# Sums of weight blocks made by adding transfers instead of VectorE

## The chip, the cores and the metric

The kernel runs on one core of a Trainium2 chip. A core has TensorE (matmuls), VectorE and ScalarE (elementwise work), GpSimd (elementwise work, and it can begin transfers), and SyncE, which here begins nearly all transfers. All transfers run on the core's 16 DMA engines. The metric is the device time of one execution in microseconds (us); lower is better. Before the change the median of three runs was 892.14 us (891.55 to 892.82).

## The reference

The program is a two-layer encoder trunk on 256 positions of 1024 channels. Each layer is a feed-forward block, a token mixer (a convolution module in the first layer, latent attention in the second) and another feed-forward block; a last norm follows.

```python
def swiglu_ffn(h, w1, w3, w2):
    return (jax.nn.silu(h @ w1) * (h @ w3)) @ w2

for i in range(DEPTH):
    h = h + 0.5 * swiglu_ffn(rmsnorm(h, ffn_norm1[i]), ffn1_w1[i], ffn1_w3[i], ffn1_w2[i])
    m = rmsnorm(h, mix_norm[i])
    h = h + (conv_module(m, ...) if i % 2 == 0 else mla(m, positions, ...))
    h = h + 0.5 * swiglu_ffn(rmsnorm(h, ffn_norm2[i]), ffn2_w1[i], ffn2_w3[i], ffn2_w2[i])
return rmsnorm(h, final_norm)
```

So there are four feed-forward blocks. The inner width is 2816. All data are float32, and `w1`, `w3`, `w2` of the four blocks are most of the bytes that are read.

## The kernel before, in words

**Weight blocks.** Weights are read in blocks of 128 partitions by 2048 float32 (1 MB). A block is loaded into one of four raw tiles (`raw`, `RAW_BUFS = 4`) by SyncE. Then it is split into two float32r tiles: `hi`, a rounded copy made by ScalarE, and `lo`, the rest `raw - hi`, made by VectorE. Each is done in two halves of 1024 columns (`PIECES = 2`). There are five pairs of `hi` and `lo` (`W_BUFS = 5`), so the splitting can run at most some four blocks ahead of TensorE. A product of float32 accuracy is three float32r matmuls (`mm3`, lines 331 to 337): rows' `hi` by weights' `lo`, `hi` by `hi`, rows' `lo` by `hi`. An ordinary block is used for two tiles of 128 rows, so it is 24 matmuls of 128x512.

**Groups of seven.** In each feed-forward block two stretches of four blocks are done in another way, by the scheme of seven products in place of eight for 2x2 blocks. One lies in chunk 3 of the up projection (an "up group", `SEVEN_UP`), one at the start of the down projection (a "down group", `SEVEN_DOWN`). That makes eight groups. The four weight blocks `four[0]` to `four[3]` are the 2x2 blocks of the weights, and the rows are cut in 2x2 blocks too: `rows(a, tb)` are plain blocks of rows, `forms[0]` to `forms[3]` are sums or differences of them, made once per group by `sums_of_rows` (line 339) and split by `forms_of`. Each of the seven products multiplies one block or form of rows by one block or sum of weight blocks, 12 matmuls, and adds it to one of four banks of results, `c11`, `c21`, `c12`, `c22`.

The weight sides are made by `load_seven` (line 190). For product `j` it says what is loaded, which sums are made, and which raw tile is split. Before the change the sums are subtractions on VectorE over a whole tile (`sub`, line 201): two at `j = 1`, one at `j = 2`, one at `j = 6`. The raw tiles 11, 12, 22, 21 are fetched at `j = 0, 0, 1, 2`, and split in the order 11, 11, 11, 21, 12, 22, 11.

`seven_products` (line 373) issues the products. Between them ScalarE copies `c11` to `c21` and one product to a spare tile `kept`, and VectorE adds `c21` and `kept` into `c12` and later into `c22`. The next product into `c21` has to wait for such a copy or add.

**What sets the order.** Every engine works through its own queue in order. The order within a queue comes from a planner that runs when the program is built. `urgent` gives instructions priority there; `order(a, b)` puts `a` behind `b`; `behind` puts a split behind the last urgent instructions. `load_ahead` says how many blocks ahead of TensorE the loads and splits are issued. SyncE's queue holds the weight loads and also the turns of the gated values (`turn_blocks`, line 480), which write 32x32-transposed tiles to memory and read them back; `gates` lists the splits of the turned values. GpSimd begins no transfer before the change; it has small norm arithmetic (lines 444 to 447) and part of the convolution.

Of the kernel before, what the change touches and what calls it, by code (L numbers as in the profile page):

```python
# [11 lines left out]
F32 = mybir.dt.float32  # L12
# [7 lines left out]
P = 128  # L20
# [69 lines left out]
def trunk(ctx: ExitStack, tc: tile.TileContext, x, xt, first, pos, invf, gfin, wdw,  # L90
# [91 lines left out]

    def fetched(src):
        raw = rawp.tile([P, HB], F32, tag="raw", name=uid("raw"))
        dma = nc.sync.dma_start(raw, src)
        if turns:
            order(dma, turns[-1].ins)
        return raw

    def load_seven(j, four, b, pieces):  # L190
        hi = wp.tile([P, HB], F32R, tag="hi", name=uid("hi"))
        lo = wp.tile([P, HB], F32R, tag="lo", name=uid("lo"))
        n = len(loaded)
        if j == 0:
            b[11], b[12] = fetched(four[0]), fetched(four[1])
        elif j == 1:
            b[22] = fetched(four[3])
        elif j == 2:
            b[21] = fetched(four[2])
        def sub(out, left, right):  # L200
            ins = nc.vector.tensor_sub(out, left, right)  # L201
            behind(ins)
            return ins

        if j == 1:
            sub(b[11], b[12], b[11])
            sub(b[12], b[22], b[12])
        elif j == 2:
            thirds[n] = sub(b[11], b[22], b[11])
        elif j == 6:  # L210
            sub(b[11], b[21], b[11])
        raw = b[(11, 11, 11, 21, 12, 22, 11)[j]]
        for i in range(pieces):
            c = slice(i * HB // pieces, (i + 1) * HB // pieces)
            casts[n, i] = nc.scalar.copy(hi[:, c], raw[:, c]), sub(lo[:, c], raw[:, c], hi[:, c].bitcast(F32))  # L215
            behind(casts[n, i][0])
        return hi, lo
# [155 lines left out]
    def seven_products(xh, xl, forms, banks, late={}):  # L373


        def rows(a, tb):
            k = slice(4 * a, 4 * a + 4)
            return xh[:, k, tbs(tb)], xl[:, k, tbs(tb)]

        def product(a, b, fresh):  # L380
            load_ahead(W_BUFS - 1)
            (hi, lo), = weights(1, False)
            for k in range(4):
# [4 lines left out]
        before = []  # L388
# [5 lines left out]
        product(forms[0], c22, True)  # L394
        kept = tmp.tile([P, 512], F32, tag="s", name=uid("p5"))
        urgent(nc.scalar.copy)(kept, c22)
        product(forms[1], c21, False)
        add = urgent(nc.vector.tensor_add)(c12, c21, kept)
        order(casts[n0 + 5, 0][1], add.ins)
        for high, low in gates[-2 * NT:-NT] if not late else ():  # L400
            order(low, thirds[n0 + 2].ins)
# [3 lines left out]
        product(rows(1, 0), c11, False)  # L405
        product(forms[2], c21, False)
        add = urgent(nc.vector.tensor_add)(c22, c21, kept)
        order(casts[n0 + 6, 0][1], add.ins)
# [3 lines left out]
        product(forms[3], c12, False)  # L412
        product(rows(1, 1), c21, False)

# [65 lines left out]
    def turn_blocks(pool, src, n, tag, after=(), b=None):  # L480
# [370 lines left out]
    def ffn_in(act, X, make_next, beside, apart, seven_up, seven_down):  # L851
# [587 lines left out]
    def mla_in(act, X, make_next, cc, sn):  # L1439
# [423 lines left out]
```

## Time and profile before

| | us |
|---|---|
| median of three runs | 892.14 |
| the profiled execution's own time | 891.44 |
| its span, first to last instruction | 889.5 |
| TensorE (PE) busy | 882.0 |
| VectorE (DVE) busy | 770.4 |
| ScalarE (ACT) busy | 580.2 |
| GpSimd (POOL) busy | 104.8 |

The mean granted TensorE clock was 0.999 of full speed. The 16 DMA engines were busy for 62% of the span and moved 198.94 MB. A group of instructions in the profile is named by its line in the kernel, the engine, the operation and the tiles it writes and reads (`out<-in`); then come the count, busy time, mean nanoseconds of one, and the idle time of the engine just before them with what ended it. Matmuls overlap in the pipeline, so the 389 ns that the profile gives a matmul of 128x512 is longer than the distance from one to the next. A stage is a stretch of the span, given in us from its start.

### The profile page before, as it was taken

What the parts mean: (1) busy time and instruction counts of PE and PEld (TensorE: products, weight loads), DVE (VectorE), ACT (ScalarE), POOL (GpSimd) and SP (SyncE); (2) the same over time, 40 slices, a digit from 0 to 9 for tenths busy, and PEclk for the clock granted to TensorE, in tenths of its full rate; (3) what the DMA queues carried; (4) which work ended last, traced back from release to release, by engine and by line L of the source; (5) the groups of instructions that cost most, each with busy time, mean ns of one, the idle gap of its engine ahead of it and who ended that gap; (6) DMA issues with size and microseconds to landing.
All of it is one profiled execution on the core that took longest, in us unless ns stands there. A gap on an engine that the chain in (4) does not pass through costs nothing.

```text
span 889.5 us, 12294 instructions
## 1 busy us (share of the span) xinstructions
PE 882.0 (99%) x4209; PEld 741.9 (83%) x4209; DVE 770.4 (87%) x1114; ACT 580.2 (65%) x1005; POOL 104.8 (12%) x227
## 2 busy tenths in 40 slices
PE   9999999999999999999999999999999999999997
PEld 7888887898988888888888888888899888888886
DVE  6899999789999998999498989995778689989973
ACT  7667868789887655657275465673676666474752
POOL 1000000079952000000010000001400010000000
PEclk9999999999999999999999999999999999999999
DMA  9884929834216855939759378495643549287541
GB/s 338 297 308 161 398 80 374 300 132 153 96 60 225 307 213 194 365 93 393 251 179 344 97 249 318 142 386 183 221 147 142 190 155 368 80 300 276 192 190 48
DMA packets 71054, 198.94 MB, mean 224 GB/s; under 512 B 12368, under 2 KB 41936, under 8 KB 51664
## 3 DMA queue, kind: packets, MB, share of 16 engines
q1 hardware_dynamic: 70560, 197.47, 61.9%
q8 instruction: 33, 0.54, 0.2%
q10 hardware_dynamic: 432, 0.69, 0.2%
q14 instruction: 29, 0.24, 0.1%
HBM read 181.87 MB, written 16.25 MB: 223 GB/s over the span
## 4 chain that ended last, share of the span: by engine, by line
PE 98%; DVE 1%; issue 0%; ACT 0%; ACTq 0%; DVEq 0%
PE u L333 17%; PE u L337 17%; PE u L336 17%; PE o L333 9%; PE o L337 9%; PE o L336 9%; PE u L1019 3%; PE gate L1019 3%; PE o L1255 3%; PE u L418 2%; PE sc L1616 1%; PE tp L453 1%; PE pairs L1062 1%; DVE lo L201 1%; PE a L337 1%; PE a L336 1%
## 5 line engine op out<-in xcount | busy, mean ns | idle before, releaser
L248 DVE TENSOR_TENSOR lo<-raw,hi 128x1024 fp32r<-128x1024 f32 (+1 forms) x228 | 266.8, 1210 | 29.2 <-ACT hi L247 28.5
L247 ACT CAST hi<-raw 128x1024 fp32r<-128x1024 f32 (+1 forms) x230 | 228.5, 1044 | 72.1 <-DMA raw<-in_f2w 24.3
L337 PE MATMUL u<-hi,Xl 128*128 128x512 f32 x592 | 230.4, 389 | 0.0
L336 PE MATMUL u<-hi,Xh 128*128 128x512 f32 x592 | 230.3, 389 | 0.0
L333 PE MATMUL u<-lo,Xh 128*128 128x512 f32 x592 | 230.2, 389 | 0.0
L215 ACT CAST hi<-raw 128x1024 fp32r<-128x1024 f32 x112 | 111.7, 1049 | 56.7 <-DVE raw L201 46.4
L201 DVE TENSOR_TENSOR lo<-raw,hi 128x1024 fp32r<-128x1024 f32 x112 | 132.0, 1215 | 6.6 <-ACT hi L215 6.5
L337 PEld LDWEIGHTS u<-hi,Xl 128*128 128x128 f32 x592 | 111.1, 188 | 23.6 <-DVE Xl L472 0.5
L336 PEld LDWEIGHTS u<-hi,Xh 128*128 128x128 f32 x592 | 111.1, 188 | 23.1
L333 PEld LDWEIGHTS u<-lo,Xh 128*128 128x128 f32 x592 | 111.1, 188 | 22.9
L333 PE MATMUL o<-lo,Gh 128*128 128x512 f32 (+1 forms) x276 | 106.7, 386 | 0.0
L336 PE MATMUL o<-hi,Gh 128*128 128x512 f32 (+1 forms) x276 | 106.5, 386 | 0.0
L337 PE MATMUL o<-hi,Gl 128*128 128x512 f32 (+1 forms) x276 | 106.5, 386 | 0.0
L444 POOL TENSOR_TENSOR ms<-ss 128x1 f32<-128x1 f32 x16 | 8.1, 509 | 592.8 <-ACT junk L436 592.8
L201 DVE TENSOR_TENSOR raw<-raw,raw 128x2048 f32<-128x2048 f32 x32 | 73.1, 2285 | 0.8 <-DMA raw<-in_f1w 0.2
L333 PEld LDWEIGHTS o<-lo,Gh 128*128 128x128 f32 x276 | 51.8, 188 | 10.6 <-DVE lo L201 0.2
L337 PEld LDWEIGHTS o<-hi,Gl 128*128 128x128 f32 x276 | 51.8, 188 | 10.5
L336 PEld LDWEIGHTS o<-hi,Gh 128*128 128x128 f32 x276 | 51.8, 188 | 10.4
L1108 DVE SCALAR_TENSOR_TENSOR acc<-V,dw,acc 128x128 f32<-128x128 f32 (+1 forms) x174 | 53.9, 390 | 0.0
L970 ACT ACTIVATE s<-u,R 128x512 f32<-128x512 f32 (+1 forms) x48 | 30.9, 647 | 29.5 <-PE u L337 28.7
L1129 ACT ACTIVATE prod<-V,dw 128x128 f32<-128x128 f32 (+1 forms) x128 | 45.6, 415 | 1.9 <-POOL Y L1130 1.0
L806 DVE SCALAR_TENSOR_TENSOR h<-o,rh,h 128x512 f32<-128x512 f32 (+1 forms) x18 | 12.9, 719 | 29.0 <-PE o L337 29.0
(269 smaller groups left out, 1306.6 us busy)
## 6 DMA issues: line engine op xcount, KB each, us to landing
raw<-in_f2w SPq DMA_DIRECT2D x66, 1024.0 KB, 5.6
raw<-in_f1w SPq DMA_DIRECT2D x62, 1024.0 KB, 6.9
raw<-in_cw SPq DMA_DIRECT2D x12, 1024.0 KB, 5.2
gd<-gt SPq DMA_DIRECT2D x160, 64.0 KB, 2.9
gb<-gd SPq DMA_DIRECT2D x24, 256.0 KB, 2.8
rows<-gd SPq DMA_DIRECT2D x16, 256.0 KB, 3.3
raw<-in_wo SPq DMA_DIRECT2D x4, 1024.0 KB, 4.7
hd<-rows SPq DMA_DIRECT2D x56, 64.0 KB, 2.3
```

The lines of the kernel that those rows point to most:

```text
L201: ins = nc.vector.tensor_sub(out, left, right)
L215: casts[n, i] = nc.scalar.copy(hi[:, c], raw[:, c]), sub(lo[:, c], raw[:, c], hi[:, c].bitcast(F32))
L247: casts[len(loaded), i] = (nc.scalar.copy(hi[:, c], raw[:, c]), low.tensor_sub(lo[:, c], raw[:, c], hi[:, c].bitcast(F32)))
L248: low.tensor_sub(lo[:, c], raw[:, c], hi[:, c].bitcast(F32)))
L333: mm = nc.tensor.matmul(o, ah, bl, start=start, stop=False, skip_group_check=seeded)
L336: nc.tensor.matmul(o, ah, bh, start=False, stop=False, skip_group_check=seeded)
L337: return nc.tensor.matmul(o, al, bh, start=False, stop=stop, skip_group_check=seeded)
L970: nc.scalar.activation(s[:, :w], u[0, tb][:, :w], AF.Silu, scale=X.r[tb])
L1019: mm = nc.tensor.matmul(u[:, t], w[:, c], X.x[:, k, t], start=(k == 0), stop=(k == KT - 1))
L1108: dve_last.append(nc.vector.scalar_tensor_tensor(out if j == j1 - 1 else y, v, w, y, op0=ALU.mult, op1=ALU.add))
L1129: prods_last.append(nc.scalar.activation(p, v, AF.Copy, scale=w))
L1255: p = nc.tensor.matmul(o[tb, d], (Zl if kind == "x" else Zh)[:, f, tbs(tb)], (lo if kind == "l" else hi)[:, c], start=(f, kind) == (0, "l" ...
```

## The change

The sums of weight blocks are no longer made by VectorE. A transfer with `accum_op=ALU.add` reads a block from memory and adds it to what lies in the raw tile; it is begun from GpSimd. Since it can only add, the signs of the row forms and of the additions of results are turned (`sums_of_rows`, `tensor_sub` in `seven_products`).

For each group four raw tiles are fetched at once, in the order d = `four[2]`, y = `four[1]`, c = `four[0]`, x = `four[0]`. Two adding transfers follow: `four[3]` to y, `four[1]` to x. At product 3 `four[3]` is added to x, at product 6 `four[2]`. At product 5 `four[3]` is loaded anew into c. The tiles are split in the order x, c, d, x, y, c, x. So a group has five plain loads where it had four, and four adding transfers where it had four subtractions.

The seven products are issued in another order, and product 2 is cut into halves, with product 3 between them. Some order rules follow the new numbering; the gated values' turns get a third buffer; and the attention's scores of heads 1 and 2 are ordered behind those of the head before.

```diff
     def load_seven(j, four, b, pieces):
...
         if j == 0:
-            b[11], b[12] = fetched(four[0]), fetched(four[1])
-        elif j == 1:
-            b[22] = fetched(four[3])
-        elif j == 2:
-            b[21] = fetched(four[2])
...
-        if j == 1:
-            sub(b[11], b[12], b[11])
-            sub(b[12], b[22], b[12])
-        elif j == 2:
-            thirds[n] = sub(b[11], b[22], b[11])
+            b["d"], b["y"], b["c"], b["x"] = (fetched(four[i]) for i in (2, 1, 0, 0))
+            nc.gpsimd.dma_start(b["y"], four[3], accum_op=ALU.add)
+            nc.gpsimd.dma_start(b["x"], four[1], accum_op=ALU.add)
+        elif j == 3:
+            nc.gpsimd.dma_start(b["x"], four[3], accum_op=ALU.add)
+        elif j == 5:
+            fetched(four[3], b["c"])
         elif j == 6:
-            sub(b[11], b[21], b[11])
-        raw = b[(11, 11, 11, 21, 12, 22, 11)[j]]
+            nc.gpsimd.dma_start(b["x"], four[2], accum_op=ALU.add)
+        raw = b["xcdxycx"[j]]
...
-        sums = [(0, x22, x21, x22, ALU.add), (2, x21, x11, x21, ALU.subtract), (1, x11, x22, x11, ALU.subtract),
-                (3, x12, x12, x11, ALU.subtract)]
+        sums = [(0, x22, x21, x22, ALU.subtract), (2, x21, x11, x21, ALU.subtract),
+                (1, x11, x22, x11, ALU.subtract), (3, x12, x12, x11, ALU.add)]
...
-        product(rows(0, 0), c11, True)
-        first = urgent(nc.scalar.copy)(c21, c11)
...
+        product(0, forms[0], c22, True)
+        kept = tmp.tile([P, 512], F32, tag="s", name=uid("p5"))
+        first = urgent(nc.scalar.copy)(kept, c22)
...
+        product(1, rows(0, 0), c11, True)
+        urgent(nc.scalar.copy)(c21, c11)
+        product(2, rows(1, 0), c11, False, range(2))
+        product(3, forms[1], c21, False)
+        product(2, rows(1, 0), c11, False, range(2, 4))
+        add = urgent(nc.vector.tensor_sub)(c12, kept, c21)
+        order(casts[n0 + 6, 0][1], add.ins)
...
+        product(4, forms[2], c21, False)
+        add = urgent(nc.vector.tensor_sub)(c22, kept, c21)
+        product(5, forms[3], c12, False)
...
+        order(casts[n0 + 7, 0][1], add.ins)
+        product(6, rows(1, 1), c21, False)
...
-            b = pool.tile([P, 512], F32, tag=tag + "b", name=uid(tag + "b"), bufs=2)
+            b = pool.tile([P, 512], F32, tag=tag + "b", name=uid(tag + "b"), bufs=3 if tag == "g" else 2)
...
-            for gate in gates[-2 * NT:]:
+            for gate in gates[-2 * NT - 1:]:
...
-            last = None
+            last = score_last[-1] if 0 < hd < 3 else None
```

More of the change, by code (lines that the diff above doesn't have):

```diff
@@ L181, in raw_to, with fetched @@
             raws[len(loaded) + len(raws)] = raw, nc.sync.dma_start(raw[:, :src.shape[-1]], src)
-    def fetched(src):
-        raw = rawp.tile([P, HB], F32, tag="raw", name=uid("raw"))
+    def fetched(src, raw=None):
+        if raw is None:
+            raw = rawp.tile([P, HB], F32, tag="raw", name=uid("raw"))
         dma = nc.sync.dma_start(raw, src)
@@ L378, in rows, with product @@
             return xh[:, k, tbs(tb)], xl[:, k, tbs(tb)]
-        def product(a, b, fresh):
+        def product(j, a, b, fresh, ks=range(4)):
             load_ahead(W_BUFS - 1)
-            (hi, lo), = weights(1, False)
-            for k in range(4):
+            if ks[0] == 0:
+                parts[j], = weights(1, False)
+            hi, lo = parts[j]
+            for k in ks:
                 c = slice(k * 512, k * 512 + 512)
@@ L387, in seven_products @@
         n0 = n_used[0]
-        before = []
+        before, parts = [], {}
         c11, c21, c12, c22 = banks[0, 0], banks[1, 0], banks[0, 1], banks[1, 1]
-        product(rows(0, 0), c11, True)
-        first = urgent(nc.scalar.copy)(c21, c11)
+        product(0, forms[0], c22, True)
+        kept = tmp.tile([P, 512], F32, tag="s", name=uid("p5"))
+        first = urgent(nc.scalar.copy)(kept, c22)
         for cast in late.values():
             order(cast, first.ins)
[L394 to L399, printed above, removed]
+        product(1, rows(0, 0), c11, True)
[5 more added lines that the diff above has]
+        order(casts[n0 + 6, 0][1], add.ins)
         for high, low in gates[-2 * NT:-NT] if not late else ():
-            order(low, thirds[n0 + 2].ins)
+            order(low, casts[n0 + 2, PIECES - 1][1].ins)
         late_gates = []
```

16 lines of the change are left out of this document (4 added, 12 removed).

## The prediction

> **What bounds the kernel now.** I read the page first, then busy time by stage, then the groups' own rows. The rows of the page, with the span, busy time by engine, the share of the chain that ended last, and the costliest groups of a weight group's work (lines L201 and L215):
>
> ```profile
> span 889.5 us, 12294 instructions
> PE 882.0 (99%) x4209; PEld 741.9 (83%) x4209; DVE 770.4 (87%) x1114; ACT 580.2 (65%) x1005; POOL 104.8 (12%) x227
> ...
> q1 hardware_dynamic: 70560, 197.47, 61.9%
> ...
> PE 98%; DVE 1%; issue 0%; ACT 0%; ACTq 0%; DVEq 0%
> ...
> L215 ACT CAST hi<-raw 128x1024 fp32r<-128x1024 f32 x112 | 111.7, 1049 | 56.7 <-DVE raw L201 46.4
> L201 DVE TENSOR_TENSOR lo<-raw,hi 128x1024 fp32r<-128x1024 f32 x112 | 132.0, 1215 | 6.6 <-ACT hi L215 6.5
> ...
> L201 DVE TENSOR_TENSOR raw<-raw,raw 128x2048 f32<-128x2048 f32 x32 | 73.1, 2285 | 0.8 <-DMA raw<-in_f1w 0.2
> ```
>
> TensorE is the bound: it is on 98% of the chain. Busy time by stage says where its 7.5 idle us (889.5 - 882.0) lie; the last columns are the granted clock, the DMA engines' share and GB/s:
>
> ```profile
> 0.00:30.00 30.00, 28.96 (x130) 23.21 (x131) 18.45 (x28) 22.42 (x37) 3.79 (x19) 1.00 0.86 322
> 90.00:110.00 20.00, 20.00 (x90) 16.57 (x89) 20.00 (x24) 17.20 (x32) 0.00 (x0) 1.00 1.02 395
> 110.00:140.00 30.00, 29.60 (x129) 23.72 (x129) 29.85 (x31) 17.71 (x22) 0.00 (x0) 1.00 0.45 152
> 353.70:389.00 35.30, 35.30 (x157) 29.22 (x156) 34.57 (x35) 20.51 (x25) 0.00 (x0) 1.00 0.77 279
> 690.00:710.00 20.00, 19.98 (x100) 16.35 (x99) 12.87 (x21) 12.39 (x29) 0.00 (x0) 1.00 0.58 211
> 860.00:889.50 29.50, 23.50 (x116) 19.75 (x114) 9.61 (x17) 6.60 (x16) 1.48 (x5) 0.98 0.10 36
> ```
>
> Of the 7.5 us, 1.04 are at the start and 6.00 at the end, which the change doesn't touch; 0.40 are inside a weight group, in this one row of TensorE's timeline:
>
> ```profile
> 136.75 0.47 PE L333 MATMUL o<-lo,rows 128*128 128x512 f32 x1 [0.40 <-DVE lo L201]
> ```
>
> VectorE is nearly as full (34.57 of 35.30 us between an up group and its down group), but its work ends in time: TensorE waited for it 0.40 us in all. So freeing VectorE can buy almost nothing; whatever makes a weight block late costs in full.
>
> **The change part by part.** One: 32 subtractions go (4 in each of 8 groups), 32 x 2.285 = 73.1 us of VectorE, 9.1 us a group. Directly worth at most the 0.40 us above.
>
> Two: SyncE begins 5 loads a group instead of 4, and GpSimd 4 adding transfers. The queue that only loads moved 395 GB/s at a share of 1.02, so 1 MB (1.049 MB) takes 1.049/395 = 2.65 us of all engines. An adding transfer also reads what it adds to: between one pass (2.65) and two (5.3). A group's DMA grows by 5 to 9 passes, 13 to 24 us; eight groups make 106 to 191 us on 61.9% of 889.5 us, so 74 to 83%. The engines still have room on average; inside a group it is tight.
>
> Three, the term that decides: the sums now lie on a chain. One buffer x is loaded, added to, cast (product 0), added to again, cast (product 3), added to again, cast (product 6). These rows are the issue of the fourth raw load of each of the eight groups, in order of time, on SyncE's queue, with the landing time of all these loads:
>
> ```profile
> 56.77 0.67 SPq L185 DMA_DIRECT2D raw<-in_f1w  x1
> 105.88 0.33 SPq L185 DMA_DIRECT2D raw<-in_f1w  x1
> 314.36 0.38 SPq L185 DMA_DIRECT2D raw<-in_f2w  x1
> 372.25 0.35 SPq L185 DMA_DIRECT2D raw<-in_f2w  x1
> 488.01 0.33 SPq L185 DMA_DIRECT2D raw<-in_f1w  x1
> 547.05 0.35 SPq L185 DMA_DIRECT2D raw<-in_f1w  x1
> 751.79 0.33 SPq L185 DMA_DIRECT2D raw<-in_f2w  x1
> 809.03 0.35 SPq L185 DMA_DIRECT2D raw<-in_f2w  x1
> ...
> DMA to landing us min/median/max: 5.3/7.6/9.5
> ```
>
> And these are the matmuls that place the groups: for the up groups (u) the first of product 1, which takes its rows from Gh; for the down groups (o) the first of product 0:
>
> ```profile
> 73.33 0.39 PE L333 MATMUL u<-lo,Gh 128*128 128x512 f32 x1
> 122.29 0.39 PE L333 MATMUL o<-lo,Gh 128*128 128x512 f32 x1
> 340.13 0.39 PE L333 MATMUL u<-lo,Gh 128*128 128x512 f32 x1
> 389.09 0.39 PE L333 MATMUL o<-lo,Gh 128*128 128x512 f32 x1
> 514.21 0.39 PE L333 MATMUL u<-lo,Gh 128*128 128x512 f32 x1
> 514.44 0.39 PE L336 MATMUL u<-hi,Gh 128*128 128x512 f32 x1
> 563.17 0.39 PE L333 MATMUL o<-lo,Gh 128*128 128x512 f32 x1
> 777.11 0.39 PE L333 MATMUL u<-lo,Gh 128*128 128x512 f32 x1
> 826.07 0.39 PE L333 MATMUL o<-lo,Gh 128*128 128x512 f32 x1
> ```
>
> Matmuls start about 0.227 us apart (514.21 to 514.44; 157 in 35.30 us give 0.225), so a product of 12 is 2.72 us and an up group starts 2.72 before its row. The lead, from the fourth load's issue to product 0, is 13.8, 23.1, 23.5 and 22.6 us for the up groups and 16.4, 16.8, 16.1 and 17.0 for the down groups. In the new order x is that fourth load.
>
> Call an adding transfer, from issue to landing, L. No row shows one. The low end is the quickest landing of these loads, 5.3; the high end the slowest plus a second pass, 9.5 + 2.65 = 12.1. I take the median landing, 7.6: the same megabyte into the same tile, on engines shared with the same traffic; a second pass on an otherwise free queue would give 5.3 + 2.65 = 8.0, close by. From x's issue to the first half cast: 7.6 (load) + L + 1.05 (ACT) + 1.22 (DVE) = 9.9 + L = 17.5. From one cast of x to the next: the rest of the cast, which must have read x, 1.2; the transfer, L; the next first half, 2.3; so 3.5 + L = 11.1 us between usable blocks. TensorE wants product 3 after 2.5 products (half of product 2 is put behind it), 6.8 us, and product 6 another 3.5 products, 9.5 us, later. A group without spare lead so loses 4.3 + 1.6 = 5.9 us; spare lead is taken off.
>
> - Up groups 2 to 4: spare 23.1 - 17.5 = 5.6, 6.0, 5.1; they lose 0.3, 0, 0.8: 1.1 us.
> - Up group 1: lead 13.8, 3.7 late already; 3.7 + 5.9 = 9.6 us.
> - Down groups: by the leads above each loses about 0.9 + 5.9 = 6.8. But the fourth buffer there came free late because VectorE was full before it (34.57 of 35.30), and 9.1 us of that goes. Leads can then grow towards the 23 us that the other up groups have. I take that, since 9.1 is more than the 6 to 7 missing: 4 x 0.4 = 1.6 us. If this cover is gone they cost 27 us.
>
> Together 12.3 us. By L = 5.3 the same sum is up group 1's 1.4 + 2.0 = 3.4 us and nothing elsewhere; by 12.1, 15 us for a group without spare lead, 14 for each of the seven others and 23 for the first: 121 us.
>
> The Trainium skill, "DMA: Bandwidth & Descriptors", section "Anatomy of one DMA", gives a transfer begun from GpSimd about 2.0 us plus bytes/436 GB/s. For 1 MB my estimate by that page is 4.4 us; the whole sum would be 1.6 us. These loads, begun from SyncE, landed in 5.3 to 9.5, which is slower, and nothing here shows an adding one.
>
> Four: what is queued behind the new waits. GpSimd's adding transfers wait for x's load and then for its casts, but GpSimd ran nothing in the stages around these groups (0.00 in 353.70:389.00), so nobody waits behind them; an issue costs about 0.3 us if like SyncE's. On SyncE the reload of c waits for product 1's casts, with the gated values' turns and the next blocks' loads behind it. Those casts run well ahead of TensorE; zero, or if they slip the next loads slip with them.
>
> Five: the half of product 2, 1.36 us, covers the copy of c21 and, behind product 3, the subtraction into c12, where a whole product covered the add before. These are the copy and the two adds in up group 2:
>
> ```profile
> 340.39 0.57 ACT L259 COPY u<-u 128x512 f32<-128x512 f32 x1 [5.64 <-PE u L337]
> ...
> 346.71 0.69 DVE L259 TENSOR_TENSOR u<-u,p 128x512 f32<-128x512 f32 x1
> 351.21 0.70 DVE L259 TENSOR_TENSOR u<-u,p 128x512 f32<-128x512 f32 x1 [0.49 <-PE u L337]
> ```
>
> Product 2 ended at 345.57 and the add at 347.40, 1.83 us later: 0.5 more than the half covers. The copy ended 0.83 after its product and the second add 0.90 after its own (351.01). So 0 to 0.5 us for each of 8 groups; I take 0.1, 1 us in all.
>
> Six: the orders given to the attention scores, the third turn buffer and the gates' order add no instruction. They cost nothing as long as TensorE has queued matmuls, as it has (19.98 of 20 us in 690:710); without that cover, tenths of a us.
>
> Sum: 891.4 (the profiled execution) - 0.4 + 12.3 + 1.0 = 904.3; the median of the runs is 0.7 higher, so **905**.
>
> **The rivals.**
> Hidden: the adding transfer takes 5 us or less, x is loaded early, and TensorE stays full. For it: only 62% of DMA time is used and three up groups have 23 us of lead. Against it: up group 1 has 13.8. Time 891 to 893. By the page's 4.4 us it would be this case, at 1.6 us.
> Faster: the one mechanism is work on VectorE and ScalarE coming earlier, so that the small delays of matmuls vanish. The rows of the attention's output product, 411 ns against 392 for its middle one:
>
> ```profile
> L333 PE MATMUL o<-lo,Oh 128*128 128x512 f32 x32 | 13.2, 411 | 0.0
> L336 PE MATMUL o<-hi,Oh 128*128 128x512 f32 x32 | 12.6, 392 | 0.0
> L337 PE MATMUL o<-hi,Ol 128*128 128x512 f32 x32 | 9.7, 411 | 0.0
> ```
>
> 64 x 0.019 = 1.2 us, and the 0.40: 1.6 us, 890.5. It decides only if all of that goes and nothing is late.
> Slow transfers: L of 10 or more, because the additions go at less than half the copying rate or wait behind loads. With L = 10, a group without spare lead loses 6.7 + 4.0 = 10.7; the first 6.1 + 10.7, seven others about 7.6: 70 us, about 962. For it: the queue was full at 1.02 just before the first down group. The same page says in "Issuing engines are not separate DMA queues" that all issuers share the 16 engines. The full stretch is loads alone, so no run here shows the sharing.
> Cover gone: L as forecast, but the down groups keep their leads of 16 to 17 us because the order of casts is kept: 905 + 27 - 2 = 930.
>
> **How the numbers follow.** Forecast 42%, hidden 22%, faster 3%, slow transfers 17%, cover gone 16%. The runs spread over 891.55 to 892.82, so about 0.2% can be told from no change: 890.4 to 893.9. Hidden falls in it but for 2 parts in 100: faster 0.03, same 0.20, slower 0.77. The likeliest case alone spans 895 to 918. The range runs from 890.8, the hidden case's edge, to 945, which leaves out the far half of the slow transfers.
>
> **What would show it.** Right: TensorE idle 12 us more, in front of products 0, 3 and 6 on L333, ended by casts whose own wait is for an adding transfer; worst in the first up group; VectorE busy some 73 us less; a GpSimd queue of 32 x 1 MB landing in about 7.6 us. Wrong: landings of 10 us and more, or stalls spread over the down groups, put it higher; TensorE busy for the same 882 us with no new idle time puts it at the old time.

## The result, and the profile after

The changed kernel takes 1020.1 us (median of 4 runs, 1016.76 to 1023.19) against 892.4 for the kernel before: a ratio of 1.143, 95% interval 1.138 to 1.148. That is 128 us slower, where 12.9 were forecast and 945 was the upper end of the range.

The profiled execution has a span of 1014.7 us. These are rows of its page: busy time by engine, the DMA queues (q0 is the new one, which GpSimd fills), and the casts to `hi` of a weight group's blocks (L209):

```profile
PE 913.4 (90%) x4209; PEld 758.3 (75%) x4209; DVE 700.6 (69%) x1082; ACT 577.7 (57%) x1005; POOL 134.7 (13%) x259
...
q1 hardware_dynamic: 71712, 205.86, 56.7%
q0 software_dynamic: 4608, 33.56, 17.3%
...
L209 ACT CAST hi<-raw 128x1024 fp32r<-128x1024 f32 x112 | 109.7, 1045 | 171.6 <-DMA raw<-in_f2w 100.7
...
raw<-in_f1w POOLq DMA_DIRECT2D x16, 1024.0 KB, 9.1
...
gd<-gt SPq DMA_DIRECT2D x160, 64.0 KB, 6.0
```

VectorE did lose its 70 us (770.4 to 700.6). But TensorE is now idle for 101.3 us (1014.7 - 913.4) where it was idle for 7.5, and it is busy for 31.4 us more with the same 4209 matmuls: 93.8 + 31.4 = 125.2, which is the whole growth of the span (1014.7 - 889.5). The casts of L209 now wait for transfers. The last row is a transfer that the change doesn't touch: the 64 KB pieces of the gated values on their way through memory. In the kernel before, the same row reads:

```profile
gd<-gt SPq DMA_DIRECT2D x160, 64.0 KB, 2.9
```

The table of waits names what ended TensorE's idle time: each row has the total, the number of times and the longest. u and o are banks of the up and down groups; L329 is the first matmul of each triple, L210 the part of the casts that makes `lo`, L255 the helper of the copies and of the sums of banks.

```profile
PE u L329 <- ACT u L255: 26.0, 4, 9.9
PE o L329 <- DVE lo L210: 24.6, 5, 6.7
PE o L329 <- ACT o L255: 21.7, 4, 8.9
PE u L329 <- DVE lo L210: 9.4, 3, 6.3
PE u L329 <- DVE u L255: 6.3, 4, 1.9
PE o L329 <- DVE o L255: 5.8, 3, 4.8
```

The six rows add up to 93.8 us: 47.7 end with ScalarE's copy of a bank, 34.0 with a cast, 12.1 with a sum of banks. The copy is short, so it must have been late. The second up group shows why. First the issues on GpSimd's queue and on SyncE's, then ScalarE, then TensorE (start, duration, in brackets the idle time before and what ended it):

```profile
348.28 0.33 SPq L186 DMA_DIRECT2D raw<-in_f2w  x1
...
355.29 0.86 POOL L199 DMA_DIRECT2D raw<-in_f2w  x1 [5.42 <-DMA raw<-in_f2w]
370.71 0.86 POOL L201 DMA_DIRECT2D raw<-in_f2w  x1 [14.56 <-DVE lo L210]
...
366.86 5.81 ACT L209 CAST hi<-raw 128x1024 fp32r<-128x1024 f32 x6 [5.08 <-DMA raw<-in_f2w]
...
379.89 1.99 ACT L209 CAST hi<-raw 128x1024 fp32r<-128x1024 f32 x2 [6.19 <-DMA raw<-in_f2w]
381.79 0.58 ACT L255 COPY p<-u 128x512 f32<-128x512 f32 x1
...
384.16 0.58 ACT L255 COPY u<-u 128x512 f32<-128x512 f32 x1
...
384.79 0.79 PE L329 MATMUL u<-lo,Xh 128*128 128x512 f32 x1 [7.43 <-ACT u L255]
385.39 0.63 PE L332 MATMUL u<-hi,Xh 128*128 128x512 f32 x1
385.81 0.63 PE L333 MATMUL u<-hi,Xl 128*128 128x512 f32 x1
```

The load of x is issued at 348.28. Its first adding transfer begins at 355.29, and the sum is cast from 366.86 on: 11.6 us. The second begins at 370.71 and ends ScalarE's wait at 379.89: 9.2 us. ScalarE works in order, and the cast of block 3 stands ahead of both copies, so the copies start only when the second adding transfer has landed (a cast of block 4 then stands ahead of the second copy). Product 2 writes the bank that the second copy reads; so TensorE stands still until 384.79.

After such a stall the matmuls are 0.43 us apart (385.39 to 385.81) instead of 0.227. The window behind this stall, with granted clock, DMA share and GB/s in the last columns:

```profile
385.00:389.00 4.00, 4.00 (x10) 3.13 (x11) 4.00 (x5) 2.18 (x3) 0.21 (x1) 0.50 0.78 116
```

The granted clock is 0.50. Behind this stall 14 matmuls go at that pace, 2.8 us more than at 0.227. Most of the 31.4 us of longer busy time lie in such stretches: in TensorE's timeline, matmuls that start over 0.3 us apart without a wait cost some 26 us more than in the kernel before. A long stall is paid for again behind it.

### The profile page after: what moved, and what is told of

Same layout as the page of the kernel before. It is cut to its first block, busy times and chain, and to the rows that moved or that the text cites. A ratio compares the mean times of both kernels' runs of the same rounds, so it can differ in the third digit from the quotient of the medians.

```text
span 1014.7 us, 12381 instructions
## 1 busy us (share of the span) xinstructions
PE 913.4 (90%) x4209; PEld 758.3 (75%) x4209; DVE 700.6 (69%) x1082; ACT 577.7 (57%) x1005; POOL 134.7 (13%) x259
## 3 DMA queue, kind: packets, MB, share of 16 engines
q0 software_dynamic: 4608, 33.56, 17.3%
## 5 line engine op out<-in xcount | busy, mean ns | idle before, releaser
L329 PE MATMUL u<-lo,Xh 128*128 128x512 f32 x592 | 233.7, 395 | 32.3 <-ACT u L255 26.0
L210 DVE TENSOR_TENSOR lo<-raw,hi 128x1024 fp32r<-128x1024 f32 x112 | 131.3, 1219 | 147.5 <-ACT hi L209 147.5
L209 ACT CAST hi<-raw 128x1024 fp32r<-128x1024 f32 x112 | 109.7, 1045 | 171.6 <-DMA raw<-in_f2w 100.7
L329 PEld LDWEIGHTS u<-lo,Xh 128*128 128x128 f32 x592 | 112.3, 190 | 58.9 <-ACT u L255 27.7
L329 PE MATMUL o<-lo,Gh 128*128 128x512 f32 (+1 forms) x276 | 109.1, 397 | 26.9 <-ACT o L255 21.7
L332 PE MATMUL o<-hi,Gh 128*128 128x512 f32 (+1 forms) x276 | 108.7, 394 | 0.0
L333 PE MATMUL o<-hi,Gl 128*128 128x512 f32 (+1 forms) x276 | 108.6, 393 | 0.0
L329 PEld LDWEIGHTS o<-lo,Gh 128*128 128x128 f32 x276 | 53.1, 192 | 40.5 <-ACT o L255 23.4
L443 POOL TENSOR_TENSOR ms<-ss 128x1 f32<-128x1 f32 x16 | 10.5, 656 | 267.2 <-ACT junk L435 267.2
L329 PE MATMUL u<-lo,Gh 128*128 128x512 f32 x64 | 28.1, 438 | 9.4 <-DVE lo L210 9.4
L971 DVE TENSOR_TENSOR s<-s,u 128x512 f32<-128x512 f32 (+1 forms) x32 | 19.6, 612 | 23.4 <-PE u L333 16.2
```

The source lines that it names most:

```text
L209: casts[n, i] = (nc.scalar.copy(hi[:, c], raw[:, c]), nc.vector.tensor_sub(lo[:, c], raw[:, c], hi[:, c].bitcast(F32)))
L210: nc.vector.tensor_sub(lo[:, c], raw[:, c], hi[:, c].bitcast(F32)))
L329: mm = nc.tensor.matmul(o, ah, bl, start=start, stop=False, skip_group_check=seeded)
L332: nc.tensor.matmul(o, ah, bh, start=False, stop=False, skip_group_check=seeded)
L333: return nc.tensor.matmul(o, al, bh, start=False, stop=stop, skip_group_check=seeded)
L443: nc.gpsimd.tensor_tensor(ms[:, 0:1], ss[:, 0:1], ss[:, 1:2], op=ALU.add)
```

## The experiments

My first theory was the forecast's own, with a larger price: the series of load, add, cast, add on the one buffer x. Rivals were the copy that ScalarE makes late, the slower clock, and the traffic as such, which delays everything else that goes through the DMA engines. Times are medians of two to ten runs, with the ratio to the kernel before and its 95% interval in brackets.

### Taking the adding transfers away, or adding nothing

Without the four adding transfers of each group (the sums are left out, everything else stays):

```diff
-            nc.gpsimd.dma_start(b["y"], four[3], accum_op=ALU.add)
-            nc.gpsimd.dma_start(b["x"], four[1], accum_op=ALU.add)
...
-            nc.gpsimd.dma_start(b["x"], four[3], accum_op=ALU.add)
...
-            nc.gpsimd.dma_start(b["x"], four[2], accum_op=ALU.add)
```

> All 32 adding transfers are left out (the sums of weight blocks are not made); the five loads a group, the new order of products and the halves of product 2 stay. Theory chain (the loss is made by the series load - add - cast - add - cast - add - cast on buffer x): nearly all of the 125 us goes, 894 to 900 us; what stays is the wait of product 2 for the copy of c11, about 0.7 us in each of 8 groups. Rival order (the new order of products and of the queues makes the loss): 940 us or more.

Measured: 905.6 us, 1.0150 [1.0133, 1.0166]. That lies between the two expectations. So 114 of the 128 us hang on the adding transfers. The other 13 are a cost of the new order alone, and TensorE's row of the second down group says where:

```profile
402.33 0.50 PE L323 MATMUL o<-lo,Gh 128*128 128x512 f32 x1 [1.38 <-ACT o L249]
```

Product 2 waits for the copy of the bank into which it goes on adding; in the up groups it does so for 0.66 to 2.12 us. In all eight groups that is 9.6 us.

The same transfers with the same bytes, copying instead of adding:

```diff
-            nc.gpsimd.dma_start(b["y"], four[3], accum_op=ALU.add)
+            nc.gpsimd.dma_start(b["y"], four[3])
```

(and so for all four)

> The 32 transfers stay on GpSimd with all their waits, but copy instead of adding (the sums are not made). If the adding itself is dear (the second pass, 2.65 us each): landings fall from about 9 to about 6.5 us, two or three steps of the chain a group, 950 to 975 us. If a transfer begun from GpSimd is slow whatever it does: landings stay at 8 to 9 us and the time above 1000 us.

Measured: 939.7 us, 1.0531 [1.0478, 1.0584]. That is below both expectations. All waits and the order of issue are as in the changed kernel, and 80 us are gone. The rows of this run on the new queue:

```profile
q0 software_dynamic: 4608, 33.56, 10.0%
...
raw<-in_f1w POOLq DMA_DIRECT2D x16, 1024.0 KB, 5.6
raw<-in_f2w POOLq DMA_DIRECT2D x16, 1024.0 KB, 6.4
```

17.3% of 1014.7 us by 32 is 5.5 us of all 16 engines for one adding transfer; 10.0% of its span of 941.6 by 32 is 2.9 for a copying one. Landing falls from 9.1 to about 6 us. This run changes two things at once, the load on the engines and the length of the series; later runs part them.

### Is it the late copy, or the series on x?

The casts of block 3 and the lower half of block 6's are put behind the copy and behind the sum of banks:

```diff
+        taken = urgent(nc.scalar.copy)(c21, c11)
+        for i in range(PIECES):
+            order(casts[n0 + 3, i][0], taken.ins)
...
+        for i in range(PIECES):
+            order(casts[n0 + 6, i][1], add.ins)
```

> The changed kernel, with ScalarE's cast of product 3 behind the copy of c21, and VectorE's part of product 6 behind the subtraction into c22. TensorE waited 47.7 us for such copies and 11.7 us for such subtractions. Theory queue (copies stuck behind casts that wait for a transfer cost their whole wait): 955 to 970 us. Theory chain (the cast that they wait behind is needed next anyway): only the half of product 2 moves into the wait, 8 to 25 us gained, 992 to 1010 us.

Measured: 1021.3 us, 1.1446 [1.1402, 1.1490]. Nothing was won; both expectations were lower. TensorE's waits for ScalarE's copies fell from 47.7 to 14.7 us, and its waits for casts rose from 34.0 to 69.8: what had been waited for behind the copy is waited for at product 3.

The same, with x loaded first and its adding transfer begun first:

```diff
-            b["d"], b["y"], b["c"], b["x"] = (fetched(four[i]) for i in (2, 1, 0, 0))
+            b["x"], b["c"], b["d"], b["y"] = (fetched(four[i]) for i in (0, 0, 2, 1))
+            nc.gpsimd.dma_start(b["x"], four[1], accum_op=ALU.add)
             nc.gpsimd.dma_start(b["y"], four[3], accum_op=ALU.add)
-            nc.gpsimd.dma_start(b["x"], four[1], accum_op=ALU.add)
```

> As copy_first, and x is fetched first instead of last and its first addition comes first in GpSimd's queue. Theory chain: the 28 us of waits in front of product 0, with the slow clock behind them, vanish, 30 to 40 us below copy_first; the waits in front of product 3 stay or grow. If the wait for x's first addition is not what makes product 0 late: no change against copy_first.

Measured: 989.8 us, 1.1093 [1.1071, 1.1115]. Loading x last costs some 31 us. Next, products 0 and 1 are exchanged, without the two orders on casts above, so that the copied bank is finished a product earlier and the copy has a whole product to itself; x is then needed a product later, too. This was run with x first and all adding transfers, and without any adding transfer and with the loads in the changed kernel's order:

```diff
-        raw = b["xcdxycx"[j]]
+        raw = b["cxdxycx"[j]]
...
-        product(0, forms[0], c22, True)
+        product(0, rows(0, 0), c11, True)
...
+        first = urgent(nc.scalar.copy)(c21, c11)
...
-        product(1, rows(0, 0), c11, True)
+        product(1, forms[0], c22, True)
...
-        urgent(nc.scalar.copy)(c21, c11)
+        urgent(nc.scalar.copy)(kept, c22)
```

> All 32 adding transfers and all sums right; products 0 and 1 in swapped places (the copy of c11 is covered, x is needed one product later) and x fetched first. Theory chain: the waits in front of the first product of x mostly go, those in front of products 3 and 6 stay: 940 to 975 us. If the waits for copies and subtractions were most of the loss: 900 to 920 us.

> As no_add (the sums of weight blocks are not made), but products 0 and 1 change places, and with them the casts: the plain rows first, so that the copy of c11 to c21 lies beside the product into c22 and not in front of product 2, which writes c11. If that copy makes what no_add still lost (13 us): 891 to 896 us. If the fifth load, the halves of product 2 or the changed queues make it: stays at 902 to 907 us.

Measured: 976.9 us with x first and all adding transfers, 1.0938 [1.0872, 1.1003]; without them 892.75 us, 1.0002 [0.9992, 1.0012]. A row of the page of the run without:

```profile
PE 882.4 (99%) x4209; PEld 741.9 (83%) x4209; DVE 701.0 (79%) x1082; ACT 579.6 (65%) x1005; POOL 106.3 (12%) x227
```

With the copy covered the new order, the fifth load, the third buffer, the orders of the attention and VectorE's 69 us less come to nothing together; singly they were not run. The 64 KB pieces take 2.9 us, as in the kernel before. This run is the floor for the rest: from it to the version with x first and all adding transfers it is 84 us. No run has x first and no transfer on GpSimd, so what that order of loads costs by itself isn't known; it is part of every difference to the floor below.

### Which of the adding transfers?

The version with x first keeps only each group's first adding transfers of x and y, or only the later two of x (the other sums are left out):

> As swap_x, without the two later additions to x (products 3 and 6 use the first sum), so 16 of 32 adding transfers are left, all of them before the group. Theory chain: the first additions lie in the lead and are mostly hidden, 893 to 910 us. If adding transfers cost by their number and traffic: about half of swap_x's loss.

> As swap_x, without the two first additions (x starts as one plain block), so the 16 adding transfers of products 3 and 6 are left. Theory chain: these lie between two casts of the same buffer and keep most of swap_x's loss, 925 to 960 us. If adding transfers cost by their number and traffic: about half of swap_x's loss, as first_add.

Measured: 925.0 us, 1.0357 [1.0321, 1.0393], and 928.6 us, 1.0397 [1.0339, 1.0454]. Over the floor 32 and 36 us for 16 transfers each, 84 for all 32. The theory of the series did not expect that of the first two, which stand at the head of a group and should have been mostly hidden; for the later two inside the group 928.6 lies in its range. That both cost the same within their intervals speaks for a price by number: 2.0 to 2.2 us for each transfer, then 2.6 with all of them.

Only y by an adding transfer, the three sums of x on VectorE as before (8 transfers, no fifth load); and the same with the second of these sums issued one block earlier:

> The same places for products 0 and 1. Only the sum y, needed for product 4, is made by an adding transfer; the three sums in x are made by VectorE with tensor_add, and there is no fifth load. All sums are right. If the series on x is what costs and not the adding transfer as such: 891 to 896 us. If each adding transfer costs the loads around it time: 900 us or more.

> As y_only, but VectorE's second sum in x is issued with product 2's weights instead of product 3's. In y_only that sum stood behind the gating multiplies of the chunk before, which end only when TensorE does. If that place made y_only's 25 us: 891 to 896 us, and an adding transfer off the series is hidden. If the adding transfer of y itself costs the time: 910 us or more.

Measured: 917.8 us, 1.0277 [1.0262, 1.0293], and 907.7 us, 1.0146 [1.0107, 1.0186]. Neither is a clean test. In the first, a weight sum of 2.27 us stands on VectorE directly ahead of the turn of a gated value (346.05 us). The second lies 15 us over the floor, between its two expectations, and its largest stalls stand behind VectorE's own queue, too, as in the fourth up group (VectorE, then TensorE; L197 is a weight sum, L212 makes `lo`):

```profile
793.86 2.25 DVE L197 TENSOR_TENSOR raw<-raw,raw 128x2048 f32<-128x2048 f32 x1
796.03 4.62 DVE L212 TENSOR_TENSOR lo<-raw,hi 128x1024 fp32r<-128x1024 f32 x4
800.57 0.69 DVE L257 TENSOR_TENSOR u<-p,u 128x512 f32<-128x512 f32 x1
...
801.31 0.50 PE L331 MATMUL u<-lo,Gh 128*128 128x512 f32 x1 [3.07 <-DVE u L257]
```

VectorE has no idle time there; a weight sum and four casts run before the sum of banks. So the 15 us, 1.9 for each of the 8 adding transfers, can't be put down to them alone.

Each adding transfer cut in two of 1024 columns, in the changed kernel:

```diff
-            nc.gpsimd.dma_start(b["x"], four[1], accum_op=ALU.add)
+            for c in (slice(0, HB // 2), slice(HB // 2, HB)):
+                nc.gpsimd.dma_start(b["x"][:, c], four[1][:, c], accum_op=ALU.add)
```

> The changed kernel with each adding transfer cut into two of 1024 columns, so that the first half can be cast while the second lands, and the next addition of a half starts after that half's cast. Theory chain (time is set by cast plus transfer, three times in series): about 4 us off each step, 940 to 985 us. If a transfer's fixed part makes its landing (two issues, each landing in 8 us or more): 1005 us or more.

Measured: 1009.4 us, 1.1310 [1.1283, 1.1337], 11 us less than the changed kernel. By the median the halves of 512 KB land after 8.6 to 8.9 us, hardly sooner than the whole megabyte (9.1 to 9.2). But the median mixes two kinds. At product 3 the whole transfer lands after 8.2 to 9.1 us and the first half after 5.4 to 6.8; the second half begins 5.7 to 7.5 us behind the first and lands 8.7 to 9.4 later. So half the bytes did land sooner, but the whole sum was ready later than with one transfer. The time lies in the second expectation's range; its reason, that each half takes 8 us or more, doesn't hold for the first halves. The run doesn't part the two theories.

### The traffic, with nobody waiting for it

The decisive run: the 32 adding transfers are begun at the same points, but into an area of memory that nobody reads (the sums are left out). A one-element copy on GpSimd ties each to the moment at which the real one could start. (Transfers into the same area also wait for one another, so some begin later.)

```diff
+    def begun(t, src, seen):
+        mark = small.tile([P, 1], F32, tag="mark", name=uid("mark"))
+        order(nc.gpsimd.dma_start(aside[t], src, accum_op=ALU.add),
+              nc.gpsimd.tensor_copy(mark, seen[:, :1]).ins)
...
+            begun("x", four[1], b["x"])
+            begun("y", four[3], b["y"])
```

> As swap_no_add with x loaded first, plus 32 adding transfers begun from GpSimd at the same points (after x's and y's loads, after the casts of x for products 1 and 3), but into a scratch area in memory that nobody reads: the traffic without the series. The products use plain blocks, so the sums are not in the result. If only the series on x costs: 893 to 898 us. If the adding transfers cost by what they take from the loads and from the turns of the gated values: 915 to 960 us.

Measured: 975.6 us, 1.0936 [1.0915, 1.0958]. Two loads that fill the area stood at the program's start and delayed its first product by 7 us, so the run was made again with the area filled just before its first use, and once more with copying transfers in place of adding ones:

> As the run traffic (products 0 and 1 exchanged, x loaded first, the 32 adding transfers at their old points into an area of memory that nobody reads; the sums are left out), but the area is first filled by two plain transfers begun from GpSimd just before the first adding one, not by two loads at the program's start. In traffic TensorE's first product began 7.0 us late (12.55 for 5.51). Traffic theory: 975.6 less some 7 to 10 us, 964 to 970. If what made traffic slow was mostly its delayed start and what followed from it: below 930.

> As traffic2, but the 32 transfers into the unread area copy instead of add (same bytes from the weights, same queue, same points; the sums are left out). Engine-time theory: a copy takes about 3 us of all engines per MB where an adding one takes 5.5, so the cost over the version without transfers is well under half of traffic2's: 905 to 920. Rival, that any 32 further megabyte transfers begun from GpSimd cost this by standing in the same engines' lists: within 10 us of traffic2.

Measured: adding 972.6 us, 1.0912 [1.0880, 1.0944], only 3 us less than with the delayed start; copying 917.4 us, 1.0276 [1.0250, 1.0301]. No engine waited for a one-element copy in either. And the copying version of the kernel with x first, where the casts do wait for the transfers:

> As swap_x, but the 32 transfers copy instead of adding (the sums are not made), in the same places and with the same waits. Series: a transfer of about 6 us gives 3.5 + 6 = 9.5 us between casts of x against the 6.8 and 9.5 us that TensorE gives; 2.7 us a group at most, 895 to 915 us. Traffic: half of the DMA time of adding ones, so about half of swap_x's 84 us, 925 to 940 us.

Measured: 913.2 us, 1.0233 [1.0212, 1.0253]. That lies in the range of the series and not in that of the traffic. But copies cost no less where nobody waits for them (917.4), so the series isn't what makes it; the theory of the traffic went wrong in taking the price as proportional to the engines' time.

So 80 of the 84 us over the floor are there although no cast waits for a sum. 25 us come with 32 more megabytes on the engines, the other 55 with the adding, which takes about twice the engine time for the same bytes. Rows of the run that adds into the unread area (L872 splits the turned values, L495 turns the gated ones):

```profile
gd<-gt SPq DMA_DIRECT2D x160, 64.0 KB, 7.0
...
ACT Gh L872 <- DMA rows<-gd: 56.6, 13, 9.4
DVE gt L495 <- DMA gd<-gt: 25.9, 7, 9.4
...
423.11:565.49 142.38, 129.47 (x554) 105.37 (x552) 91.09 (x112) 73.39 (x104) 9.83 (x15) 0.97 0.82 264
```

and of the run without any, the stage from the second down group to the third up group:

```profile
388.64:513.99 125.35, 125.35 (x554) 103.53 (x552) 95.50 (x117) 72.92 (x102) 5.86 (x8) 1.00 0.71 251
```

The same 554 matmuls take 142.4 us instead of 125.4, at a DMA share of 0.82 instead of 0.71: the engines are not full on average, yet a transfer of 64 KB takes 7.0 us instead of 2.9 (medians over the whole run). This landing time alone doesn't give the price. The run that copies into the unread area is 55 us faster and has

```profile
gd<-gt SPq DMA_DIRECT2D x160, 64.0 KB, 5.9
...
DVE gt L495 <- DMA gd<-gt: 4.2, 3, 2.3
```

The waits behind it differ far more: VectorE's for a gt buffer (4.2 us instead of 25.9), and ScalarE's for the loads of ordinary weight blocks (36.3 us without any transfer, 65.0 with copying, 118.8 with adding ones). How the delay reaches TensorE is seen at the second down group of the run that adds into the unread area: GpSimd's issues, SyncE's, VectorE's work, TensorE's.

```profile
419.02 0.81 POOL L200 DMA_DIRECT2D asidey<-in_f2w  x1 [0.36 <-issue]
...
422.81 11.61 SPq L504 DMA_DIRECT2D gb<-gd  x2
...
434.14 0.45 DVE L495 STREAM_TRANSPOSE gt<-s 128x256 f32<-128x256 f32 x1 [9.39 <-DMA gd<-gt]
...
440.22 0.69 DVE L266 TENSOR_TENSOR o<-p,o 128x512 f32<-128x512 f32 x1
...
441.06 0.77 PE L340 MATMUL o<-lo,rows 128*128 128x512 f32 x1 [6.62 <-DVE o L266]
```

Adding transfers begin at 419.02 and, in a row not shown, at 420.21. The turns behind them drag, VectorE stands 9.39 us before a gt buffer (the turned gated value on the chip) that has not been read yet, its casts and the sum of banks start that much later, and TensorE loses 6.62 us. Nothing in this chain reads a weight sum.

A third gt buffer (taken from the turned values, gb) takes a part of that wait away:

```diff
-        t = pool.tile([P, 512], F32, tag=tag + "t", name=uid(tag + "t"), bufs=2)
+        t = pool.tile([P, 512], F32, tag=tag + "t", name=uid(tag + "t"), bufs=3 if tag == "g" else 2)
...
-            b = pool.tile([P, 512], F32, tag=tag + "b", name=uid(tag + "b"), bufs=3 if tag == "g" else 2)
+            b = pool.tile([P, 512], F32, tag=tag + "b", name=uid(tag + "b"), bufs=2)
```

> As traffic2 (the 32 adding transfers go into an area of memory that nobody reads; the sums are left out), with three instead of two buffers for the gated values that wait for their turn through memory (gt), and two instead of three for the turned ones (gb). In traffic2 VectorE stood 35.1 us before a gt buffer whose transfer had not been read yet. If TensorE's stalls come from that wait: 972.6 falls by 15 to 35 us, to 940 to 957. If they come from the splits of the turned values (ScalarE 56.6 us before Gh, VectorE 48.9 us behind it): within 10 us of traffic2, 963 to 983.

Measured: 959.1 us, 1.0725 [1.0682, 1.0769], 13.5 less and between the two expectations. Rows of its table of waits:

```profile
ACT Gh L872 <- DMA rows<-gd: 62.4, 11, 13.5
...
PE u L340 <- DVE s L266: 20.8, 3, 8.3
...
PE o L340 <- DVE o L266: 4.3, 3, 2.9
```

The stalls before the down groups' sums fell from 21.3 us to 4.3: these did come from the gt buffer. Those of the up groups stayed (15.4, now 20.8); they stand behind the split of the turned values, for which ScalarE waits just as long as before. So both waits carry the delay to TensorE. A third way is the loads: in the run that adds into the unread area, stalls of 8.4 and 6.9 us end with casts of ordinary blocks, the first of them behind a wait of ScalarE of 16.4 us for a load of 1 MB. That load was begun at 83.64 and landed 18.6 us later; three adding transfers, begun at 79.52, 83.73 and 89.86, ran beside it, and the DMA share from 84 to 103 us is 1.01. How much each way costs by itself was not parted further.

### The slow clock

45 matmuls of nothing ahead of product 2 in the last six groups, to keep TensorE busy through the stall:

```diff
...
+            for _ in range(45):
+                mm = nc.tensor.matmul(idle[:, :256], still[:, :P], still, start=True, stop=True)
...
```

> The changed kernel with 45 idle matmuls of 128x256 bfloat16 (about 5 us) in front of product 2 in the last six groups, where TensorE waited 5.8 to 9.9 us for the copy. If the idle time itself slows the matmuls behind it (0.43 us apart instead of 0.23 for some 14 of them): the slow stretch there goes, 2 to 3 us in each of six groups, 1000 to 1010 us. If the slow matmuls have another cause: no gain or a loss, 1015 us or more.

Measured: 1041.2 us, 1.1667 [1.1640, 1.1693], worse by 21. At the place itself it did what it should:

```profile
385.64 0.50 PE L329 MATMUL u<-lo,Xh 128*128 128x512 f32 x1 [2.59 <-ACT u L255]
385.98 0.39 PE L332 MATMUL u<-hi,Xh 128*128 128x512 f32 x1
386.21 0.40 PE L333 MATMUL u<-hi,Xl 128*128 128x512 f32 x1
```

With 2.59 us of idle time instead of 7.43 the matmuls behind it are 0.34 and then 0.23 us apart. But the waits came back elsewhere, above all before the sums of banks: 19.1 us on the up groups' sums, where the changed kernel had 6.3. The slow clock is a consequence of the stalls, and what it costs by itself was not settled by this run.

## Why the prediction was wrong

Its direction held, its size didn't. The steps, by their numbers:

**One, VectorE's 73 us are worth nothing: right.** Without adding transfers and with the copy covered the time is 892.75, with VectorE at 701.0 us.

**Two, the DMA engines: the sum was near, the conclusion wrong.** The adding transfer takes 5.5 us of all engines, two passes. The two queues' time grew by 200 us (from 61.9% of 889.5 to 74.0% of 1014.7), just above the forecast's 106 to 191; that the share stayed at 74% is owed to the longer span. "The engines still have room on average" was true and beside the point.

**Three, the series on x: a mis-sized term, and not the one that decides.** L was taken as 7.6 us; the median is 9.1 to 9.2, and it is 11.6 and 9.2 in the second up group. That lies inside the forecast's bounds, and by its own formula an L of 10 to 12.1 gives 962 to about 1013 us. Such a number would have been near for the wrong reason: the run that adds into the unread area has no series at all and takes 972.6. The load of x ahead of it can also take longer than 7.6; the one in the first row below landed after 12.8:

```profile
417.53 0.50 SPq L186 DMA_DIRECT2D raw<-in_f2w  x1
...
431.11 0.86 POOL L199 DMA_DIRECT2D raw<-in_f2w  x1 [12.12 <-DMA gd<-gt]
...
440.03 5.78 ACT L209 CAST hi<-raw 128x1024 fp32r<-128x1024 f32 x6 [21.29 <-DMA raw<-in_f2w]
442.38 0.80 PE L329 MATMUL o<-lo,s1h 128*128 128x512 f32 x1 [6.48 <-DVE lo L210]
```

These are SyncE, GpSimd, ScalarE and TensorE of the changed kernel before the second down group. From the load's issue to product 0 it is 24.9 us (417.53 to 442.38), of which 13.6 passed until the adding transfer's issue and 8.9 until the cast. But 6.48 of it is TensorE's stall: TensorE was free for product 0 after 18.4 us. In the four down groups that lead is 17 to 18 us, where the kernel before had 16 to 17. The growth towards 23 us, by which the forecast gave these groups 1.6 us, did not come: their stalls in front of product 0 are 21.9 us together (4.08, 6.48, 4.62, 6.72). On that point the rival of the gone cover was right. Put on top of the traffic, the waits for the sums cost 4 us with x first (972.6 to 976.9), which can't be told from noise, and some 30 more with x last, against 12.3 forecast.

**Four, what is queued behind the waits: the step that failed.** It asked who waits behind GpSimd, found nobody, and put the step at zero. It never asked who else uses the engines that the transfers occupy. "If they slip the next loads slip with them" had the right neighbours, for the wrong reason: it is the turns and loads themselves that slow down. With x first the step was worth 80 us, by the runs into the unread area. (An issue on GpSimd took 0.86 us, too, instead of about 0.3.) The Trainium skill, "DMA: Bandwidth & Descriptors", section "Issuing engines are not separate DMA queues", says that transfers of all issuers interleave on the same 16 engines; the forecast used it for the adding transfers' own landing and not for what the others would lose. The runs into the unread area show the sharing: 2.9 us become 7.0 for a 64 KB piece begun from SyncE.

**Five, the half of product 2 covers the copy: wrong.** Product 2 goes on adding into c11, the very bank that the copy reads, so it waits for it and covers nothing. Forecast 1 us; without any adding transfers it was 13 (905.6 against 892.75, products 0 and 1 exchanged).

**Six, the remaining orders at nothing: borne out,** as far as the sum of all at 892.75 shows it.

The rival "hidden" used the price that the Trainium skill gives in "DMA: Bandwidth & Descriptors", section "Anatomy of one DMA"; the forecast's estimate by it was 4.4 us for a megabyte begun from GpSimd. By their medians copying ones landed in 5.6 to 6.4 us beside the changed kernel's loads (up to 9.3 in other runs) and adding ones in 9.1 to 9.2, so the measurement decides against it.

Laid end to end, from the floor up: 25 us for 32 more megabytes (892.75 to 917.4), 55 for their adding (to 972.6), 4 for waiting for the sums (to 976.9, within the noise of the two runs), 13 for the copy without cover (to 989.8), 30 for loading x last (to 1020.1). These are differences of neighbouring runs, so their sum is no check. The exchange of products 0 and 1 is worth 13 us at both ends, with the adding transfers (976.9 to 989.8) and without them (892.75 to 905.6); with them it also gives x a product more of time, and the run at 989.8 has its own orders on casts, so the agreement may be partly chance. The terms overlap all the same: copying instead of adding is worth 80 us in the changed kernel and 64 with x first (976.9 to 913.2). And the writes of the unread area go to memory and not into a buffer on the chip, so its 80 us need not be exactly the share that the real transfers' traffic has. Nor do they say which stalls of the changed kernel are the traffic's: there most of TensorE's idle time ends with casts of weight sums or with copies held up behind them, and such a wait contains both the series and the slower transfers.

## What to carry to other kernels

Work that moves from an engine off the critical path onto the DMA engines can be paid by every other transfer: ask first which queues wait in order for the others, the small ones and the loads, and only then for the share of busy time. An addition made by a transfer took about twice the engines' time of a copy here, and in a kernel whose loads already use 62% of them it cost 80 us where nobody waited for it; where the engines stand idle was not tried. And before half a product is counted as cover for a copy, see which bank that product writes.

## What the runs showed of the hardware

- An adding transfer of 1 MB took 5.3 to 5.9 us of all 16 engines (17.5% of 979.3 us for the 32 of the version with x first, 5.2% of 907.6 for the 8 of the last run with y alone), a copying one from the same issuer 2.7 to 2.9 (9.6% of 911.3 us and 10.0% of 941.6, by 32). The Trainium skill, "Collectives: The Full Stack", section "The bandwidth ceiling: the fold count and why AG ≠ RS ≠ AR", gives as the reason for a slower reduction that an add reads two sources; a factor of about 2 agrees with that.
- At product 3, an adding transfer of 1 MB landed after 8.2 to 9.1 us, a copying one after 4.9 to 5.3, and the first half of a halved adding one (512 KB) after 5.4 to 6.8.
- The granted clock fell to 0.50 behind long stalls, but the length of the stall did not fix it. In the run that copies into the unread area a stall of 2.82 us is followed by slow matmuls at once, 0.43 us apart, and one of 3.61 by two gaps of 0.34 and 0.31 us before the slow ones:

```profile
348.81 0.79 PE L340 MATMUL u<-lo,Gh 128*128 128x512 f32 x1 [2.82 <-DVE s L266]
349.40 0.63 PE L343 MATMUL u<-hi,Gh 128*128 128x512 f32 x1
...
812.57 0.50 PE L340 MATMUL u<-lo,Gh 128*128 128x512 f32 x1 [3.61 <-DVE u L266]
812.91 0.52 PE L343 MATMUL u<-hi,Gh 128*128 128x512 f32 x1
813.22 0.63 PE L344 MATMUL u<-hi,Gl 128*128 128x512 f32 x1
```

The Trainium skill, "TensorE: Matmul & The Clock Gate", section "What's actually happening", says that the clock is halved after an idle window of about 3.4 us and that the windows run freely. The half clock and the varying onset agree; the 2.82 us stall is shorter than the window that it states.
